# A ConvFFN over 2176 tokens: blocks of 724, 726 and 726 tokens become blocks of 868, 870 and 438

## The chip, the cores and the metric

One core of one Trainium2 chip runs the whole kernel in one launch. The metric is the device time of that launch in microseconds (us); smaller is better. Each execution of a kernel gives one time, and one further execution is profiled.

## The reference

One step of a one-layer encoder over 2048 prompt tokens and 8 x 16 sample tokens (2176 columns together), width 1024, in float32. Only the end of it is touched:

```
mix = concat(RMSNorm(A), RMSNorm(B)) @ w_out ;  x += RMSNorm(mix)
up = RMSNorm(x) @ w_up                 # 1024 -> 2 x 2816
up_c = causal depthwise conv (width 3) of up, + bias
f = (gelu(up_c[:2816]) * up_c[2816:]) @ w_down      # 2816 -> 1024
x += RMSNorm(f)
```

## The kernel before

Activations lie with features on the 128 partitions and tokens along the free axis, so a matmul takes a 128x128 weight tile as the stationary operand and a chunk of tokens as columns of the moving one. Each float32 operand is split into a high and a low part, and a product is three matmuls (hi·hi, lo·hi, hi·lo; `mm3`, L266 to L269). Every weight tile goes through `weights` (L174): a DMA from the SP queue into `wr` (two buffers), a cast on ScalarE (ACT) to `whi` (L184), a subtraction on VectorE (DVE) to `wlo` (L185); three weight buffers, two jobs of prefetch.

The stages are: the input projection with chunks of 384 and 512 columns; attention and gating; the output projection of six pieces of up to 384 tokens (48 jobs, `psm`); the ConvFFN. In the output projection two of the eight weight tiles (`KEEP`) stay resident over all six pieces, and the others are loaded again for each. For pieces 0 and 1 a chain there (`h2_chain`) also makes the normed input `hhi`, `hlo` of the first FFN block.

The FFN runs three blocks one after the other. A block has 44 up jobs (22 gate tiles, 22 value tiles, interleaved; 8 k-steps, two column chunks, three matmuls each) and down jobs in groups: when the 22 products `g` of a group are there, each of the 8 output tiles `m` adds its partial sum into `acc` (`down`, L1116). A job's two chunks go into the two `pd` buffers of PSUM, and DVE adds them into `acc` (L1139), so that the job after next needs these adds. The last up job of a block is followed by three down jobs of the fourth group and the eight of the last.

The input of block 1 and of block 2 is made by `ffn_prep_chain` (L871): first sums of squares, long ahead; then, once the last up job no longer reads `hhi`, for each sub-chunk of 182 columns a load of x1 into the single buffer `xp` (L880), eight products on DVE (L899), eight casts on ACT (`hhi`, L902), eight subtractions (`hlo`, L903), half on DVE and half on GpSimd (POOL). The next sub-chunk's load must wait until the last subtraction has read `xp`. The result of a block is normed, added to x1 (`xr`) and stored by `y_chain`, while the next block's up jobs run; the last block has `y_last_chain`, with its last group split into 470 and 256 columns so that the first part's chain runs beside the second part's matmuls.

A list scheduler lays out each engine's instructions from the program's order and its own estimates; each engine then runs its own list strictly in order.

Of the kernel before, what the change touches and what calls it, by code (L numbers as in the profile page):

```python
# [53 lines left out]
def hybrid_kernel(ctx: ExitStack, tc: tile.TileContext, a: dict):  # L54
# [194 lines left out]
    def sq_step(pool, key, acc, src, first, n, eng=None):  # L249
# [3 lines left out]
        else:  # L253
            sq = pool.tile([P, TAIL if key == "y" else 384], F32, tag="sq1" + key, name="sq1", bufs=2)
# [616 lines left out]
    def ffn_prep_chain(pool, pspool, fb, out, free):  # L871

        s0, n0, n1 = FBLK[fb]
        subs = [(o, min(182, n0 + n1 - o)) for o in range(0, n0 + n1, 182)]
        rbs = pool.tile([P, 728], F32, tag="rbs", name="rbs", bufs=1)
# [17 lines left out]
        hhi = hpool.tile([P, KD, 728], F32R, tag="hhi", name="hhi")  # L893
        hlo = hpool.tile([P, KD, 728], F32R, tag="hlo", name="hlo")
        for i, (off, n) in enumerate(subs):
            x, nxt = nxt, fetch_x1(*subs[i + 1]) if i + 1 < len(subs) else None
            for k in range(KD):
# [5 lines left out]
                (nc.gpsimd if k % 2 else nc.vector).tensor_tensor(out=lo, in0=x[:, k, :n], in1=hi.bitcast(F32),  # L903
                                                                  op=ALU.subtract)
# [6 lines left out]
    with ExitStack() as c3:  # L911
# [34 lines left out]
        def x1_chain(pi, mix, acc):  # L946
# [13 lines left out]
            if pi < 2:  # L960
                sumb = two.tile([P, 384], F32, tag="dgb", name="sumb", bufs=1)
            for k in range(KD):
# [10 lines left out]
                if pi < 2:  # L973
                    sq_step(two, "x", sumb, mix[:, k, :n], k == 0, n, nc.vector)
            held.discard("x")
            if pi < 2:
                chains.append(h2_chain(pi, mix, sumb))

        def h2_chain(pi, mix, acc):
# [5 lines left out]
            rb = (yield from rstd_chain(two, ps3s, "b", acc, n, D))[1]  # L985
# [47 lines left out]
        KEEP = (0, 2)  # L1033
        h2 += [hpool.tile([P, KD, 728], F32R, tag=t, name=t) for t in ("hhi", "hlo")]
# [14 lines left out]
    with ExitStack() as c4:  # L1049
# [8 lines left out]
        C0 = 150  # L1058
        NT = 726

        def block_jobs(fb, h2, h2n):
            s0, n0, n1 = FBLK[fb]
            first = fb == 0
            st = {}

            def up(f, w):
# [5 lines left out]
                segs = [(ps[:, 512 - n0:512], 0, n0), (ps[:, 512:512 + n1], n0, n1)]  # L1072
# [5 lines left out]
                if f == 2 * NF - 1:  # L1078
                    st["up"] = True
                    if h2n is None:  # L1080
                        x = st["x"] = hpool.tile([P, KD, 728], F32R, tag="hhi", name="xl").bitcast(F32)
# [5 lines left out]
                y = (ypool if first and f == 0 else two).tile([P, NT], F32, tag="yg" if f < NF else "yv", name="y")  # L1087
# [28 lines left out]
            def down(f0, G, m, parts, w):  # L1116
                dhi, dlo = w
                if f0 == 0 and m == 0:
                    st["acc"] = one.tile([P, KD, NT], F32, tag="acc", name="acc")
# [13 lines left out]
                for pi, pd, c in zip(parts, pds, cs):  # L1133
# [6 lines left out]
                    if last:  # L1140
                        if m == 0:
                            st["sum", pi] = one.tile([P, TAIL], F32, tag=f"sumy{pi}", name="sumy")
# [176 lines left out]
```

## Time and profile before

| | |
|---|---|
| three timed runs | 2992.3, 2996.45, 2998.28 us; median 2996.45 us |
| profiled execution | 2994.85 us, its span 2993.1 us (1.75 us lie around the span) |
| mean granted TensorE clock | 0.986 of full |
| TensorE (PE) busy | 2865.8 us, 96% of the span |
| FFN in the span | from about 1378 us to the end |
| weight tiles loaded | output projection 38, up 132, down 120 |

Span means from the first instruction to the last. PE's busy time counts a stretch as busy while a matmul is anywhere in its pipeline; matmuls overlap, so the distance from one start to the next, not the length of one, says what a matmul costs.

### The profile page before, as it was taken

How to read it: one execution, taken by the hardware profiler on the slowest of the kernel's cores; microseconds unless marked ns; L12 is line 12 of the kernel's file. 1: busy time of each engine (PE TensorE's matmuls, PEld its weight loads, DVE VectorE, ACT ScalarE, POOL GpSimd, SP SyncE). 2: the span in 40 equal slices, each digit the busy share in tenths (PEclk: the TensorE clock that was granted, in tenths of full speed). 3: DMA queues.
4: the chain of work that ended last, by engine and by line, in shares of the span. 5: the costliest groups of instructions: out<-in, count | busy, mean ns of one | idle time of the engine just before them, and what ended most of it. 6: DMA issues, size and time to landing. Idle time of an engine off the chain costs nothing.

```text
span 2993.1 us, 44225 instructions
## 1 busy us (share of the span) xinstructions
PE 2865.8 (96%) x17070; PEld 2620.6 (88%) x17070; DVE 1899.7 (63%) x2848; ACT 1354.4 (45%) x2399; POOL 343.1 (11%) x487
## 2 busy tenths in 40 slices
PE   8999978889999988999999999999999999999997
PEld 7999766567676657999999999899999999999997
DVE  6666658887988895876544555763444476344445
ACT  5444447777777774554332233433232243323222
POOL 0000011110111121552000000310000030000002
PEclk9999989999999999999999999999999999999998
DMA  7766864333424326665222212442212233211223
GB/s 241 243 232 232 253 205 127 117 100 82 120 85 113 106 60 205 211 206 184 79 68 72 64 61 75 150 123 76 69 50 71 63 111 117 77 58 59 75 64 109
DMA packets 241521, 360.26 MB, mean 120 GB/s; under 512 B 26400, under 2 KB 171040, under 8 KB 240288
## 3 DMA queue, kind: packets, MB, share of 16 engines
q1 hardware_dynamic: 241312, 357.44, 38.6%
q8 instruction: 135, 2.21, 0.3%
q14 instruction: 74, 0.61, 0.1%
HBM read 289.85 MB, written 67.51 MB: 119 GB/s over the span
## 4 chain that ended last, share of the span: by engine, by line
PE 56%; DVE 3%; DMA 2%; issue 1%; ACT 1%; POOL 0%; SPq 0%; POOLq 0%; DVEq 0%; ACTq 0%
PE pu L268 12%; PE pu L269 12%; PE pu L267 12%; PE pd L267 5%; PE pd L268 5%; PE pd L269 5%; PE psm L267 2%; PE psm L269 2%; PE psm L268 1%; DMA xp<-x_s 1%; DMA wr<-wout 1%; DVE xp L899 1%; DVE wlo L185 0%; PE rb L209 0%; PE rb L236 0%
## 5 line engine op out<-in xcount | busy, mean ns | idle before, releaser
L185 DVE TENSOR_TENSOR wlo<-wr,whi 128x1024 fp32r<-128x1024 f32 (+2 forms) x333 | 364.1, 1094 | 575.8 <-ACT whi L184 573.4
L267 PE MATMUL pu<-hhi,whi 128*128 128x364 f32 (+1 forms) x2112 | 694.8, 329 | 1.0 <-ACT nhs L1103 1.0
L268 PE MATMUL pu<-hlo,whi 128*128 128x364 f32 (+1 forms) x2112 | 695.5, 329 | 0.0
L269 PE MATMUL pu<-hhi,wlo 128*128 128x364 f32 (+1 forms) x2112 | 694.9, 329 | 0.0
L184 ACT CAST whi<-wr 128x1024 fp32r<-128x1024 f32 (+2 forms) x333 | 305.1, 916 | 726.3 <-PE pu L268 275.5
L267 PEld LDWEIGHTS pu<-hhi,whi 128*128 128x128 f32 x2112 | 398.6, 189 | 1.5 <-ACT nhs L1103 1.5
L268 PEld LDWEIGHTS pu<-hlo,whi 128*128 128x128 f32 x2112 | 398.0, 188 | 0.4 <-POOL hlo L903 0.3
L269 PEld LDWEIGHTS pu<-hhi,wlo 128*128 128x128 f32 x2112 | 397.5, 188 | 0.1
L267 PE MATMUL pd<-ghi,whi 128*128 128x362 f32 (+3 forms) x1016 | 335.2, 330 | 12.2 <-DVE acc L1139 11.5
L269 PE MATMUL pd<-ghi,wlo 128*128 128x362 f32 (+3 forms) x1016 | 334.1, 329 | 0.0
L268 PE MATMUL pd<-glo,whi 128*128 128x362 f32 (+3 forms) x1016 | 334.1, 329 | 0.0
L1091 DVE SCALAR_TENSOR_TENSOR y<-pu,cvec,y 128x726 f32<-128x726 f32 (+2 forms) x352 | 269.9, 777 | 8.7 <-ACT y L1088 4.1
L535 DVE TENSOR_TENSOR_SCAN S<-S 128x896 f32<-128x896 f32 (+8 forms) x136 | 216.3, 1594 | 24.4 <-ACT S L532 23.9
L532 ACT ACTIVATE S<-z 128x512 f32<-128x512 f32 (+4 forms) x336 | 189.0, 566 | 69.8 <-PE z L669 24.8
L686 PEld LDWEIGHTS pt<-ident,s 128*128 128x128 f32 x1088 | 126.6, 145 | 93.5 <-issue 34.8
L669 PE MATMUL z<-K,Q 128*128 128x512 f32 (+3 forms) x640 | 199.1, 408 | 8.7 <-ACT s L533 6.5
L267 PEld LDWEIGHTS pd<-ghi,whi 128*128 128x128 f32 x1016 | 191.9, 189 | 15.9 <-DVE acc L1139 8.0
L686 PE MATMUL pt<-ident,s 128*128 128x128 f32 x1088 | 176.8, 288 | 28.3 <-ACT wT L687 15.9
L1139 DVE TENSOR_TENSOR acc<-acc,pd 128x362 f32<-128x362 f32 (+2 forms) x192 | 101.5, 530 | 154.9 <-PE pd L269 154.3
L537 DVE TENSOR_TENSOR s<-s,S 128x640 f32<-128x640 f32 (+7 forms) x200 | 179.3, 901 | 27.6 <-ACT s L533 13.8
L268 PEld LDWEIGHTS pd<-glo,whi 128*128 128x128 f32 x1016 | 191.7, 189 | 0.3
L269 PEld LDWEIGHTS pd<-ghi,wlo 128*128 128x128 f32 x1016 | 191.4, 188 | 0.3
(210 smaller groups left out, 4913.8 us busy)
## 6 DMA issues: line engine op xcount, KB each, us to landing
wr<-wup SPq DMA_DIRECT2D x132, 512.0 KB, 3.3
wk<-win_t SPq DMA_DIRECT2D x96, 256.0 KB, 2.7
wr<-win_f SPq DMA_DIRECT2D x48, 512.0 KB, 5.3
wr<-wout SPq DMA_DIRECT2D x38, 512.0 KB, 3.9
wr<-wdown SPq DMA_DIRECT2D x72, 256.0 KB, 2.7
Q<-q_s SPq DMA_DIRECT2D x128, 128.0 KB, 5.1
x<-xT SPq DMA_DIRECT2D x40, 384.0 KB, 5.2
wr<-wdown SPq DMA_DIRECT2D x48, 320.0 KB, 2.9
```

The source lines that it names most:

```text
L184: nc.scalar.copy(hi, wr)
L185: nc.vector.tensor_tensor(out=lo, in0=wr, in1=hi.bitcast(F32), op=ALU.subtract)
L267: nc.tensor.matmul(ps, lhsT=whi, rhs=ahi, start=start, stop=False)
L268: nc.tensor.matmul(ps, lhsT=whi, rhs=alo, start=False, stop=False)
L269: nc.tensor.matmul(ps, lhsT=wlo, rhs=ahi, start=False, stop=stop)
L532: nc.scalar.activation(S[:, c0:c0 + cn], z, AF.Sigmoid, scale=-1.0)
L535: nc.vector.tensor_tensor_scan(out=R, data0=R, data1=R, initial=1.0 if carry is None else carry, op0=ALU.mult, op1=ALU.bypass)
L537: nc.vector.tensor_tensor(out=s[:, :W], in0=s[:, :W], in1=S[:, 1:W + 1], op=ALU.mult)
L669: nc.tensor.matmul(z, lhsT=Q[:, j, i * P:(i + 1) * P], rhs=K2[:, b0 * P + c0:b0 * P + c0 + cn], start=(j == 0), stop=(j == 1 and not diago ...
L686: nc.tensor.transpose(pt[:, j], st["w"][:, (j0 - b0 + j) * P:(j0 - b0 + j + 1) * P], ident)
L1091: nc.vector.scalar_tensor_tensor(out=o, in0=i, scalar=w, in1=o, op0=ALU.mult, op1=ALU.add)
L1139: nc.vector.tensor_tensor(out=o, in0=o, in1=src, op=ALU.add)
```

## The change

The FFN's blocks become 868, 870 and 438 tokens wide. In columns that PE multiplies by (with two halo or pad columns in each block) they are 434 + 436, 436 + 436 and 440 in a single chunk; before they were 362 + 364, 364 + 364 and 364 + 364. Both make 2182 columns. The down projection goes in six groups (4, 4, 4, 4, 3, 3 tiles) instead of five (5, 5, 4, 4, 4). The wider tiles take room: the gate's output `yg` has one buffer instead of two, `g` six instead of eight, `xr` three instead of four, and one output weight tile stays resident instead of two. Since the first block is wider, piece 2 of the output projection also makes 100 columns of its input. The prep's sub-chunks are five of 176 (the last 168) for block 1 and three of 148 (the last 144) for block 2, and all of `hlo` is made on POOL. The last group's parts are 256 and 182 columns.

```diff
-FBLK = [(0, 362, 364), (722, 364, 364), (1448, 364, 364)]
+FBLK = [(0, 434, 436), (866, 436, 436), (1736, 440, 0)]
+WB = 872
-FGROUPS = [5, 5, 4, 4, 4]
+FGROUPS = [4, 4, 4, 4, 3, 3]
-TAIL = 470
+TAIL = 256
+WY = 436
...
-        subs = [(o, min(182, n0 + n1 - o)) for o in range(0, n0 + n1, 182)]
+        total = n0 + n1
+        step = 2 * -(-total // (2 * -(-total // 182)))
+        subs = [(o, min(step, total - o)) for o in range(0, total, step)]
...
-                (nc.gpsimd if k % 2 else nc.vector).tensor_tensor(out=lo, in0=x[:, k, :n], in1=hi.bitcast(F32),
-                                                                  op=ALU.subtract)
+                nc.gpsimd.tensor_tensor(out=lo, in0=x[:, k, :n], in1=hi.bitcast(F32), op=ALU.subtract)
...
-            if pi < 2:
+            if pi < 3:
                 chains.append(h2_chain(pi, mix, sumb))
...
-        KEEP = (0, 2)
+        KEEP = (0,)
...
-                segs = [(ps[:, 512 - n0:512], 0, n0), (ps[:, 512:512 + n1], n0, n1)]
+                segs = [(ps[:, base:base + n0], 0, n0)] + ([(ps[:, 512:512 + n1], n0, n1)] if n1 else [])
...
-                y = (ypool if first and f == 0 else two).tile([P, NT], F32, tag="yg" if f < NF else "yv", name="y")
+                y = (ypool if f < NF else two).tile([P, WB - 2], F32, tag="yg" if f < NF else "yv", name="y")[:, :NT]
...
-                    st["g", f - NF] = split(two, y, [P, NT], "g", bufs=8)
+                    ghl = [two.tile([P, WB - 2], F32R, tag="g" + t, name="g" + t, bufs=6)[:, :NT] for t in ("hi", "lo")]
...
-                CS = [slice(0, 362), slice(362, NT)]
+                CS = [slice(0, n0), slice(n0, NT)] if n1 else [slice(0, NT)]
...
-                    xr = two.tile([P, 364], F32, tag="xr", name="xr", bufs=4)
+                    xr = two.tile([P, WY], F32, tag="xr", name="xr", bufs=3)
```

What the scheduler makes of it is seen where the first block ends and the second's input is prepared. On DVE, before, from one product of the second sub-chunk (`xp`) to the first products of the third, with `acc` the adds that free a `pd` buffer:

```order
L899 SCALAR_TENSOR_TENSOR xp<-xp,cvec,rbs 128x182
L1139 TENSOR_TENSOR acc<-acc,pd 128x364
L903 TENSOR_TENSOR hlo<-xp,hhi 128x182
L899 SCALAR_TENSOR_TENSOR xp<-xp,cvec,rbs 128x182
L185 TENSOR_TENSOR wlo<-wr,whi 128x512
L903 TENSOR_TENSOR hlo<-xp,hhi 128x182
L899 SCALAR_TENSOR_TENSOR xp<-xp,cvec,rbs 128x182
L1139 TENSOR_TENSOR acc<-acc,pd 128x362
L1139 TENSOR_TENSOR acc<-acc,pd 128x364
L185 TENSOR_TENSOR wlo<-wr,whi 128x512
L1139 TENSOR_TENSOR acc<-acc,pd 128x362
L899 SCALAR_TENSOR_TENSOR xp<-xp,cvec,rbs 128x182 x4
```

In the changed kernel, on DVE, from the second sub-chunk of the five to the third:

```order
L1147 TENSOR_TENSOR acc<-acc,pd 128x434
L904 SCALAR_TENSOR_TENSOR xp<-xp,cvec,rbs 128x176 x8
L1147 TENSOR_TENSOR acc<-acc,pd 128x436
L188 TENSOR_TENSOR wlo<-wr,whi 128x384
L1147 TENSOR_TENSOR acc<-acc,pd 128x434
L1147 TENSOR_TENSOR acc<-acc,pd 128x436
L188 TENSOR_TENSOR wlo<-wr,whi 128x384
L1147 TENSOR_TENSOR acc<-acc,pd 128x434
L1147 TENSOR_TENSOR acc<-acc,pd 128x436
L904 SCALAR_TENSOR_TENSOR xp<-xp,cvec,rbs 128x176 x8
```

The subtractions have left DVE, and the eight products of a sub-chunk stand together; from one sub-chunk's start to the next there are five `acc` adds, where before there were four. Counting on in the same list, there are five from the third to the fourth sub-chunk and three from the fourth to the fifth, which follows the block's last add.

On POOL, at the same place, the last three rows of the prep in the changed kernel with what stands around them (`sumy` is the sum of squares of the block's result, `rstd` its reciprocal root, which needs the block's last down job):

```order
L908 TENSOR_TENSOR hlo<-xp,hhi 128x176 x8
L259 TENSOR_TENSOR sumy<-sumy,sq_18842 128x436
L219 TENSOR_TENSOR rstd<-var,mhalf 128x4
L908 TENSOR_TENSOR hlo<-xp,hhi 128x168 x8
L219 TENSOR_TENSOR rstd<-var,mhalf 128x2
```

Before, the last rows there were these:

```order
L903 TENSOR_TENSOR hlo<-xp,hhi 128x182 x3
L256 TENSOR_TENSOR sumy<-sumy,sq_18605 128x362
L903 TENSOR_TENSOR hlo<-xp,hhi 128x182
L256 TENSOR_TENSOR sumy<-sumy,sq_18609 128x364
L216 TENSOR_TENSOR rstd<-var,mhalf 128x3
```

The fifth sub-chunk now stands behind the `rstd` of the finished block; before, the last sub-chunk was ahead of it.

On PE, the end of the first block before (`pd` are down jobs; `pu` are up jobs, here of the second block):

```order
L269 MATMUL pd<-ghi,wlo 128x362
L267 MATMUL pu<-hhi,whi 128x364
L267 MATMUL pd<-ghi,whi 128x364
L268 MATMUL pd<-glo,whi 128x364
```

And in the changed kernel, with the sums of squares of the finished block (`rb<-ones,sumy`):

```order
L271 MATMUL pd<-glo,whi 128x436
L272 MATMUL pd<-ghi,wlo 128x436
L272 MATMUL pu<-hhi,wlo 128x436
L212 MATMUL rb<-ones,sumy 128x64 x4
L270 MATMUL pu<-hhi,whi 128x436 x2
```

Before, up matmuls of the second block over all of its columns stood ahead of the last down jobs. Now only those over its first 436 columns do, and the first that read the second 436 columns (the last row shown) follow the `sumy` matmuls.

## Rows read from the trace of the kernel before

**Rows 1.** The page: the span.

```profile
span 2993.1 us, 44225 instructions
```

**Rows 2.** Windows in the FFN, PE alone: busy, matmuls, granted clock, DMA.

```profile
1500.00:1800.00 300.00, 300.00 (x1802) 1.00 0.22 66
2000.00:2400.00 400.00, 400.00 (x2406) 1.00 0.22 67
2500.00:2900.00 400.00, 400.00 (x2403) 1.00 0.23 72
```

**Rows 3.** Groups by shape, PE: count of the first of three matmuls.

```profile
L267 PE MATMUL pu<-hhi,whi 128*128 128x364 f32 x1760 | 578.4, 329 | 0.0
...
L267 PE MATMUL pd<-ghi,whi 128*128 128x364 f32 x496 | 164.0, 331 | 5.9 <-DVE acc L1139 5.9
...
L267 PE MATMUL pu<-hhi,whi 128*128 128x362 f32 x352 | 116.4, 331 | 1.0 <-ACT nhs L1103 1.0
```

**Rows 4.** Timeline of PE, last group: 34 starts at 470 columns, 36 at 256.

```profile
2953.49 0.37 PE L269 MATMUL pd<-ghi,wlo 128*128 128x470 f32 x1
...
2960.59 0.38 PE L269 MATMUL pd<-ghi,wlo 128*128 128x470 f32 x1
2960.80 0.28 PE L267 MATMUL pd<-ghi,wl 128*128 128x256 f32 x1
...
2964.98 0.28 PE L269 MATMUL pd<-ghi,wl 128*128 128x256 f32 x1
```

**Rows 5.** Timeline of PE, earlier stages: 55 starts at 512 columns; 97 at 384.

```profile
99.29 0.39 PE L396 MATMUL pst<-wklo,hhi 128*128 128x512 f32 x1
...
111.53 0.39 PE L396 MATMUL pst<-wklo,hhi 128*128 128x512 f32 x1
...
118.13 0.33 PE L267 MATMUL psf<-hhi,whi 128*128 128x384 f32 x1
...
134.77 0.34 PE L267 MATMUL psf<-hhi,whi 128*128 128x384 f32 x1
```

**Rows 6.** Timeline of PE in the gating stage: eight starts at 512 columns.

```profile
923.18 0.40 PE L820 MATMUL pu<-uw,xl 128*128 128x512 f32 x1
...
924.80 0.40 PE L818 MATMUL pu<-uw,xh 128*128 128x512 f32 x1
```

**Rows 7.** Who PE waited for in the FFN: us, times, longest.

```profile
PE pd L267 <- DVE acc L1139: 11.5, 9, 2.7
```

**Rows 8.** Windows at the two block borders, PE alone.

```profile
1850.00:1910.00 60.00, 53.55 (x317) 1.00 0.42 123
2385.00:2450.00 65.00, 59.28 (x351) 1.00 0.33 102
```

**Rows 9.** Timelines of SP and DVE at the first border: load, landing, next load.

```profile
1865.52 0.38 SPq L880 DMA_DIRECT2D xp<-x_s  x1
...
1877.97 0.38 SPq L880 DMA_DIRECT2D xp<-x_s  x1
...
1870.36 1.64 DVE L899 SCALAR_TENSOR_TENSOR xp<-xp,cvec,rbs 128x182 f32<-128x182 f32 x4 [1.11 <-DMA xp<-x_s]
```

**Rows 10.** All subtractions of the prep by engine: shortest, median, longest in ns.

```profile
L903 DVE TENSOR_TENSOR hlo<-xp,hhi x32: 331/341/741, 1853.5 to 2440.6; 128x182 fp32r<-128x182 f32 x32
L903 POOL TENSOR_TENSOR hlo<-xp,hhi x32: 505/582/1559, 1854.6 to 2442.6; 128x182 fp32r<-128x182 f32 x32
```

**Rows 11.** Output projection: window (PE, PEld, DVE, ACT, POOL busy), then instructions added to it.

```profile
1158.00:1378.00 220.00, 214.67 (x1288) 209.39 (x1288) 158.52 (x249) 113.54 (x218) 115.36 (x108) 0.99 0.63 211
...
L185 DVE TENSOR_TENSOR wlo<-wr,whi x37: 1208/1226/2037, 1169.4 to 1370.7; 128x1024 fp32r<-128x1024 f32 x37
...
L256 DVE TENSOR_TENSOR sumb<-sumb,sq x14: 545/560/1365, 1205.0 to 1259.8; 128x384 f32<-128x384 f32 x14
```

**Rows 12.** The page's DMA issues: down weights, KB each, us to landing.

```profile
wr<-wdown SPq DMA_DIRECT2D x72, 256.0 KB, 2.7
```

**Rows 13.** The last window: PE, PEld, DVE, ACT, POOL busy, clock, DMA.

```profile
2973.00:2993.10 20.10, 2.85 (x15) 1.90 (x13) 15.70 (x31) 0.74 (x2) 7.96 (x10) 0.61 0.40 148
```

More of the change, by code (lines that the diff above doesn't have):

```diff
@@ L892, in ffn_prep_chain @@
             yield
-        hhi = hpool.tile([P, KD, 728], F32R, tag="hhi", name="hhi")
-        hlo = hpool.tile([P, KD, 728], F32R, tag="hlo", name="hlo")
+        hhi = hpool.tile([P, KD, WB], F32R, tag="hhi", name="hhi")
+        hlo = hpool.tile([P, KD, WB], F32R, tag="hlo", name="hlo")
         for i, (off, n) in enumerate(subs):
@@ L984, in h2_chain @@
             yield
-            rb = (yield from rstd_chain(two, ps3s, "b", acc, n, D))[1]
+            rb = (yield from rstd_chain(two, ps3s, "b", acc, max(n, P), D))[1]
             parts = [(0, 0, NSAMP), (NSAMP, NSAMP + 2, n - NSAMP)] if pi == 0 else [(0, c0 + 2, n)]
@@ L1031, in wout @@
             return resident[m]
-        KEEP = (0, 2)
-        h2 += [hpool.tile([P, KD, 728], F32R, tag=t, name=t) for t in ("hhi", "hlo")]
+        KEEP = (0,)
+        h2 += [hpool.tile([P, KD, WB], F32R, tag=t, name=t) for t in ("hhi", "hlo")]
         for t in h2:
@@ L1064, in block_jobs @@
             st = {}
+            NT = n0 + n1 if first else n0 + n1 - 2
+            base = 512 - n0 if n1 else 0
+            C0 = base if first else base + 2
             def up(f, w):
@@ L1118, in down @@
                 if f0 == 0 and m == 0:
[L1119 removed]
+                    st["acc"] = one.tile([P, KD, WB - 2], F32, tag="acc", name="acc")
                 acc = st["acc"]
                 last = f0 + G == NF
[L1122 removed]
+                CS = [slice(0, n0), slice(n0, NT)] if n1 else [slice(0, NT)]
                 if last and h2n is None:
@@ L1141, in down @@
                         if m == 0:
-                            st["sum", pi] = one.tile([P, TAIL], F32, tag=f"sumy{pi}", name="sumy")
+                            st["sum", pi] = one.tile([P, WY], F32, tag=f"sumy{pi}", name="sumy")
                         sq_step(two, "y", st["sum", pi], o, m == 0, n, nc.vector if m == KD - 1 else None)
@@ L1147, in down_job @@
             def down_job(f0, G, m):
-                return (lambda: weights(a["wdown"][m][:, f0:f0 + G])), (lambda w: down(f0, G, m, (0, 1), w))
+                return (lambda: weights(a["wdown"][m][:, f0:f0 + G])), (lambda w: down(f0, G, m, (0, 1) if n1 else (0,), w))
             def last_job(f0, G, m, pi):
@@ L1168, in y_last_chain @@
                 x, t0 = st["x"], s0 + 2 + c0
-                rb = (yield from rstd_chain(one, psd, "yb"[pi], ssum, n, D, w=(TAIL, 256)[pi]))[1]
+                rb = (yield from rstd_chain(one, psd, "yb"[pi], ssum, n, D, w=TAIL))[1]
                 for k in range(KD):
@@ L1185, in y_chain @@
                 yield from lock("y")
-                rb = (yield from rstd_chain(one, psd, "y", ssum, n, D, w=TAIL))[1]
+                rb = (yield from rstd_chain(one, psd, "y", ssum, n, D, w=WY))[1]
                 if first:
```

19 lines of the change are left out of this document (10 added, 9 removed).

## The prediction

> **What bounds the kernel now.** The windows come first: three undisturbed stretches of the FFN, 1100 us of the span [rows 1], in which PE is busy all the time at the full granted clock [rows 2]. They hold 1802 + 2406 + 2403 = 6611 starts, so a matmul costs 1100/6611 = 166.4 ns there from one start to the next. The reader is to see that nothing but the number of matmuls and this distance sets the FFN's time. The groups by shape give the number: 1760 + 352 = 2112 first matmuls of up jobs [rows 3], three matmuls each, so 6336; the down jobs are 22 tiles x 8 outputs x 3 matmuls x 2 chunks x 3 blocks = 3168 (496 of the first kind at 364 columns in the same rows, as many at 362, and 64 in the last split). Together 9504 at 363.6 columns. At 2.4 GHz, the level that the granted clock of 1.00 stands for, 363.6 columns are 151.5 ns, so 14.9 ns of a matmul do not go by columns. Next the list of waits: what PE loses in the FFN is mostly the wait of down jobs for `acc`, 11.5 us in nine waits [rows 7], and the windows put the loss at the two block borders: 60 - 53.55 = 6.45 us and 65 - 59.28 = 5.72 us, 12.2 together [rows 8].
>
> **The change part by part.**
>
> *Fewer, wider matmuls.* The columns stay (2182 for up, 2178 for down), the matmuls fall: up 44 x 24 x 5 = 5280, down 22 x 24 x 5 = 2640, and 72 more for the split of the last group: 7992, or 1512 fewer. No row has 436 columns, so the distance is bounded by its neighbours. At 470 columns it is 7.10 us/33 = 215.2 ns, at 256 4.18/35 = 119.4 ns [rows 4]. At 512 it is 12.24/54 = 226.7 ns, at 384 16.64/96 = 173.3 ns [rows 5], but at 512 in the gating stage 1.62/7 = 231.4 ns [rows 6]. Less the columns at 2.4 GHz these are 19.3 ns at 470, 12.8 at 256, 13.3 at 512 and 384, 18.1 at 512 in gating: the part that does not go by columns is no constant. It is smallest where chunk and tile sizes are multiples of 64 columns, and largest at the wide odd ones. 436 is odd, so I lean to that side. For 435.9 columns the mean is then: 195.0 ns with 13.3 ns; 196.5 with the 14.9 of now; 198.1 on the line from 166.4 at 363.6 to 231.4 at 512; 199.6 on the line to 215.2 at 470; 201.0 with the 19.3 of 470. I take 198.1. Before: (9504 - 192) x 0.1664 + 96 x 0.2152 + 96 x 0.1194 = 1581.6 us. After: (7992 - 144) x 0.1981 + 72 x 0.1194 + 72 x 0.09 = 1569.8 us (182 columns lie between 182/2.4 = 75.8 ns and the 119.4 of 256; the middle). **-12 us**, ends -36 (195.0) and +11 (201.0).
>
> The Trainium skill, TensorE: Matmul & The Clock Gate, section Back-to-back issue gap, gives the isolated distance as columns/2.4 plus 2.5 ns; by it 1512 fewer matmuls would return 3.8 us. The distances above do not agree with it: what stands beside the columns is 13 to 19 ns here, so its figure is not used.
>
> *Block borders.* At the first border a load of `xp` goes out at 1865.52 us, its first product starts at 1870.36, and the next load goes out at 1877.97 [rows 9]: a sub-chunk takes 12.4 us, of which 4.8 are the load. DVE's list puts the first product of a sub-chunk ahead of `acc` adds, so while DVE waits for the load, PE runs out of `pd` buffers. Between two such products there were four adds, two down jobs of 24 x 0.1664 = 4.0 us: 12.4 against 8.0. Now there are five adds, 2.5 jobs of 18 x 0.198 = 3.6 us = 8.9 us, and a sub-chunk is a little shorter in loading (176 columns). What grows is the number of sub-chunks for block 1, five for four, with 11 down jobs beside them that last 11 x 3.6 = 39 us instead of 44. All subtractions now run on POOL: 8 x 0.582 = 4.7 us a sub-chunk, where DVE did four at 0.341 [rows 10]; with the load (4.8) and a first product and cast ahead (about 1, an estimate from the 0.4 us that a product takes in the same row group 9: four in 1.64) that is 10.5 us, and more where `sumy` adds stand between. I walk it: from the end of the last up job (0), loads go out at about 15 (as before, DVE has the tile's last elementwise work first), 25, 35.5 and 46.5; the waits of PE for `acc` are about 3.0, 2.2 and 0.8 us; the fifth sub-chunk lands at 51, and its first `hlo` is there at about 52, where the down jobs and the six matmuls ahead of the second half of the columns would have ended at 41 without any wait. So about 11 us are lost at the first border, 4.5 more than now. At the second border there are three sub-chunks: loads at about 12 and 22, waits of 3.7 and 2.4 us, and the third is there long before the down jobs end: 6.1 against 5.7. **+5 us**; below, 0 (the longer DVE list hides it as well as now); above, +13 (the fifth sub-chunk at 12.4 us each and not at 10.5: four times 1.9 us more).
>
> *Output projection.* One more weight tile loaded for five pieces: 5 x 1.23 us on DVE. Eight more squares and sums at 0.56 us each, and 100 columns of `h` and `hlo` for eight k. DVE is busy 158.5 of 220 us and PE 214.7 [rows 11], so PE has 5.3 us of idle time there and DVE 61 us of room for some 6 + 4.5 + 4 us. **+2 us**; ends 0 (all in the room) and +8 (half of the added DVE work delays a weight tile).
>
> *Third block.* One chunk, so an up job lasts 24 x 0.2 = 4.8 us and a down job 12 x 0.2 = 2.4 us, where a down job had 4 to 5 us. A down tile needs 2.7 us from issue to landing [rows 12], and two `wr` buffers and two jobs of lead (4.8 us) cover it. The one place where it is thin is the first down group, beside which SP also issues the loads and stores of `xr` for the second block, now with three buffers. **+1 us**; ends 0 and +8 (eight jobs short by 1 us).
>
> *Tail.* After the last matmul come 20.1 us, of which DVE works 15.7 [rows 13]. The last block's parts shrink from 470 and 256 columns to 256 and 182, so its elementwise work shrinks by 438/726, but the second part's matmuls hide 6.5 us of it instead of 11.5: 15.7 x 0.4 = 6.3 less, 5.0 more, **-2 us** with the shorter chain of four pieces instead of six; ends 0 and -5.
>
> *At nothing:* the single gate buffer (a value job's product on DVE is done many us before the next gate tile's 48 matmuls end, cover 9.5 us, and 4.8 in the third block), six `g` buffers (3 + 3 or 4 + 1 tiles live), 24 more down loads of the same total bytes.
>
> Sum: -12 + 5 + 2 + 1 - 2 = -6 us. The profiled execution took 2994.85, so 2989; the median of the timed runs lies 1.6 above it: **2990 us**.
>
> **The rivals.**
>
> *The width pays in full.* If the part beside the columns stays at the 14.9 ns of now, or falls to 13.3, the first term is -24 to -36, and with the rest at +6 the kernel takes 2979 to 2967. For it: 362 and 364 are odd too and have no more. Against: 470 and 512 in gating. Chance 0.20.
>
> *The width pays nothing* (the other side). If 436 columns cost like 470 (199.6 to 201.0 ns), the first term is 0 to +11 and the kernel takes 3002 to 3013; it decides from about 199.4 ns on. For it: 470 is the nearest wide row. Against: those are 96 matmuls of one place. Chance 0.17.
>
> *The fifth sub-chunk becomes the border.* POOL's subtractions go up to 1.56 us [rows 10] and the last sub-chunk stands behind `rstd`, so each step may take 12.4 us or more; at +13 to +20 for the border the kernel takes 2998 to 3005. The Trainium skill, GPSIMD Engine Reference, section Engine selection, advises VectorE for two-input elementwise work and puts GpSimd at about twice its time; the medians above, 582 to 341 ns, bear it out at 1.7. Chance 0.13.
>
> *The change doesn't reach PE:* short jobs of the third block starve (weights late by 1 us in each of 24 down jobs or more), which eats the gain: 2998 to 3010. For it: two loads in flight only; against: all three stages of a tile take less than its lead. Chance 0.10.
>
> **How the numbers follow.** The forecast (a net of -2 to -12) has 0.40. A measurement of this kernel tells 0.2%, 6 us, from no change; the forecast lies at that edge, so half of its chance is faster and half the same. Faster is 0.20 and the first rival's 0.20. Of the other three a part ends within 6 us: same is 0.20 + 0.06 + 0.06 + 0.04 = 0.36, slower 0.11 + 0.07 + 0.06 = 0.24. The range leaves out the ends of the first rival below and of the second and fourth above: 2973 to 3004. The forecast's own range is 2984 to 2994.
>
> **What the profile after would show.** Windows inside the blocks with 100/0.198 = 505 starts in 100 us (513 if the first rival holds, 498 if the second); 5280 up and 2712 down matmuls in three lines; PE losing about 11 us at the first border, the last piece of it on `hhi` or `hlo` of the fifth sub-chunk, and about 6 at the second; 43 output weight tiles; a last window of some 18 us. Wrong I would be above all by the distance at 436 columns: a nanosecond there is 7.8 us.

## The result

The changed kernel takes 3021.02 us (median of 4 timed runs, 3015.88 to 3024.86), the kernel before 2994.38 us beside it: ratio 1.0081, 95% interval 1.0069 to 1.0093, or +24 us. The forecast was 2990 with a range up to 3004, so it missed in direction and by 31 us. The profiled execution took 3024.86 us, the slowest of the four; its span is 30.0 us longer than that of before [rows 1].

The page of the changed kernel, span and DMA issues (KB each, us to landing):

```profile
span 3023.1 us, 41499 instructions
...
wr<-wdown SPq DMA_DIRECT2D x96, 256.0 KB, 2.7
wr<-wout SPq DMA_DIRECT2D x43, 512.0 KB, 4.6
...
wr<-wdown SPq DMA_DIRECT2D x48, 192.0 KB, 2.4
```

Windows of the changed kernel, PE alone (busy, starts, granted clock, DMA), in undisturbed stretches of the FFN, to be read against [rows 2]:

```profile
1500.00:1900.00 400.00, 400.00 (x2023) 1.00 0.20 60
2100.00:2600.00 500.00, 500.00 (x2531) 1.00 0.21 63
2760.00:2940.00 180.00, 180.00 (x901) 1.00 0.36 107
```

The reader is to see the cadence: 400/2023 and 500/2531 are 197.7 ns per start, 180/901 (440 columns) 199.8. The forecast was 198.1. The wide matmuls do what was said of them, and the loss must lie elsewhere.

Windows of the same kernel at the two borders, the first jobs of the third block, the last group, and behind the last matmul (the last row has PE, PEld, DVE, ACT and POOL):

```profile
1960.00:2060.00 100.00, 87.52 (x400) 0.90 0.35 104
2610.00:2680.00 70.00, 63.47 (x321) 1.00 0.26 75
2680.00:2750.00 70.00, 64.72 (x324) 1.00 0.60 185
2975.00:3009.00 34.00, 30.15 (x199) 0.95 0.32 101
...
3009.00:3023.00 14.00, 1.69 (x7) 1.10 (x6) 9.64 (x29) 0.71 (x2) 5.81 (x10) 0.66 0.38 128
```

At the first border there are 400 starts in 100 us; at 197.7 ns they are worth 79 us, so 21 us are gone, and only 12.5 of them are idle time. Most of the rest (6.0 us, by the table below) stands in the clock: 0.90, where [rows 8] have 1.00. The lists of waits of PE in the output projection, at the first border, at the second with the third block's start, and in the last group (us, times, longest):

```profile
PE psm L270 <- ACT mix L1020: 4.4, 2, 2.3
PE rb L239 <- DVE dg L231: 4.2, 3, 1.9
...
PE pd L270 <- DVE acc L1147: 10.3, 4, 3.3
PE pu L270 <- ACT hhi L907: 1.3, 1, 1.3
PE rb L212 <- DVE sumy L259: 0.9, 1, 0.9
...
PE pd L270 <- DVE acc L1147: 6.5, 3, 2.7
PE pu L270 <- ACT nhp L1110: 2.6, 2, 1.6
PE pd L270 <- ACT acc L1145: 1.7, 1, 1.7
...
PE pd L270 <- ACT wl L187: 3.5, 3, 2.2
```

The timeline of DVE at the first border: the eight products of sub-chunks 2 to 5, and one of the adds behind them.

```profile
1990.27 5.21 DVE L904 SCALAR_TENSOR_TENSOR xp<-xp,cvec,rbs 128x176 f32<-128x176 f32 x8 [0.48 <-DMA xp<-x_s]
1995.40 0.59 DVE L1147 TENSOR_TENSOR acc<-acc,pd 128x436 f32<-128x436 f32 x1
...
2003.80 4.56 DVE L904 SCALAR_TENSOR_TENSOR xp<-xp,cvec,rbs 128x176 f32<-128x176 f32 x8
...
2018.11 5.76 DVE L904 SCALAR_TENSOR_TENSOR xp<-xp,cvec,rbs 128x176 f32<-128x176 f32 x8 [0.23 <-DMA xp<-x_s]
...
2031.78 3.84 DVE L904 SCALAR_TENSOR_TENSOR xp<-xp,cvec,rbs 128x168 f32<-128x168 f32 x8 [0.30 <-DMA xp<-x_s]
```

A sub-chunk takes 13.5, 14.3 and 13.7 us from one to the next, where the prediction walked with 10.5. The timeline of PE beside it:

```profile
1996.05 0.48 PE L270 MATMUL pd<-ghi,whi 128*128 128x436 f32 x1 [3.31 <-DVE acc L1147]
...
1998.14 0.57 PE L270 MATMUL pd<-ghi,whi 128*128 128x436 f32 x1
1998.50 0.57 PE L271 MATMUL pd<-glo,whi 128*128 128x436 f32 x1
...
2000.69 0.36 PE L270 MATMUL pd<-ghi,whi 128*128 128x434 f32 x1
2000.88 0.36 PE L271 MATMUL pd<-glo,whi 128*128 128x434 f32 x1
...
2009.86 0.55 PE L270 MATMUL pd<-ghi,whi 128*128 128x434 f32 x1 [3.02 <-DVE acc L1147]
...
2032.59 1.09 PE L270 MATMUL pu<-hhi,whi 128*128 128x436 f32 x2 [1.31 <-ACT hhi L907]
```

PE waits 3.3 us until the eight products let the add through, and then its matmuls start 0.36 us apart (1998.14 to 1998.50), at the lower of the two clock levels, before they are back at 0.19. The second half of the columns starts at 2032.59, when the fifth sub-chunk's `hhi` is there.

To add this up by place, the trace of each kernel was read in one way: for each FFN matmul, the distance to the next start less the usual one for its columns (columns at 2.4 GHz plus 15 ns), where that is over 40 ns. In brackets is the part in matmuls at the lower clock level. The output projection is the time from the start of the last matmul of the stage ahead to that of its own last.

| us | vs before | output proj. | FFN start | border 1 | border 2 | third block's start | last group | after the last matmul |
|---|---|---|---|---|---|---|---|---|
| before | | 223.8 | 2.2 | 8.7 (0.0) | 7.4 (0.0) | 0.3 | 0.8 | 19.4 |
| changed | +24 | 231.0 | 5.4 | 22.6 (6.0) | 9.6 (0.0) | 5.1 | 7.8 (1.6) | 14.3 |
| before, POOL alone | +8 | 225.4 | 2.3 | 13.3 (3.0) | 12.4 (2.7) | 0.3 | 0.7 | 19.1 |
| before, reload alone | +4 | 230.2 | 4.1 | 8.3 (0.0) | 9.7 (1.5) | 0.3 | 0.7 | 19.0 |
| before, groups alone | +26 | 224.7 | 2.1 | 18.1 (2.5) | 16.3 (2.7) | 0.3 | 6.7 (1.7) | 19.1 |
| changed, old widths | +26 | 226.9 | 5.3 | 18.6 (4.5) | 16.3 (2.9) | 0.3 | 6.6 (1.6) | 19.0 |
| changed, half on DVE | +29 | 230.0 | 3.1 | 22.1 (2.3) | 11.2 (1.5) | 8.2 | 10.1 | 14.8 |
| changed, 16 jobs | +18 | 230.0 | 3.2 | 17.6 (5.5) | 6.4 (1.5) | 7.4 | 7.4 | 14.5 |
| changed, two `xp` | +13 | 229.6 | 5.4 | 11.0 (0.0) | 7.2 (0.0) | 5.1 | 7.7 | 14.5 |
| changed, all three | +4 | 231.9 | 3.0 | 7.4 (0.3) | 4.5 (0.2) | 7.2 | 7.1 | 14.5 |
| old widths, all three | +10 | 225.2 | 3.2 | 13.7 (0.0) | 8.5 (0.0) | 0.3 | 4.9 | 19.0 |
| before, 16 jobs, two `xp` | -14 | 225.1 | 2.3 | 4.1 (0.0) | 1.2 (0.0) | 0.6 | 1.0 | 18.8 |

Of the 30.0 us between the spans 3.9 lie ahead of the output projection, where the code is the same (that point was reached at 1131 to 1144 us in all profiles). The FFN, from the last matmul of the output projection to the last of its own, grew from 1612.7 to 1636.7: +24.0, of which stalls are 52.3 - 20.3 = +32.0, so the matmuls themselves gave back 8.0.

### The profile page after: what moved, and what is told of

Its sections match the earlier page's. It is cut to its first block, busy times and chain, and to the rows that moved or that the text cites. A ratio compares the mean times of both kernels' runs of the same rounds, so it can differ in the third digit from the quotient of the medians.

```text
span 3023.1 us, 41499 instructions
## 1 busy us (share of the span) xinstructions
PE 2881.4 (95%) x15566; PEld 2549.3 (84%) x15566; DVE 1926.9 (64%) x2886; ACT 1364.9 (45%) x2436; POOL 367.8 (12%) x524
## 4 chain that ended last, share of the span: by engine, by line
PE 51%; DVE 5%; DMA 4%; ACT 1%; issue 1%; POOL 1%; SPq 0%; DVEq 0%; POOLq 0%; ACTq 0%
PE pu L271 11%; PE pu L270 11%; PE pu L272 11%; PE pd L270 5%; PE pd L272 5%; PE pd L271 5%; DVE wlo L188 1%; DMA wr<-wout 1%; DVE xp L904 1%; DMA xp<-x_s 1%; PE psm L270 1%; PE psm L272 1%; PE psm L271 1%; ACT whi L187 1%; DVE mix L967 1%
## 5 line engine op out<-in xcount | busy, mean ns | idle before, releaser
L270 PE MATMUL pu<-hhi,whi 128*128 128x434 f32 (+2 forms) x1760 | 636.7, 362 | 6.0 <-ACT nhp L1110 2.6
L271 PE MATMUL pu<-hlo,whi 128*128 128x434 f32 (+2 forms) x1760 | 638.0, 362 | 0.0
L272 PE MATMUL pu<-hhi,wlo 128*128 128x434 f32 (+2 forms) x1760 | 636.5, 362 | 1.1 <-DVE wlo L188 1.1
L270 PE MATMUL pd<-ghi,whi 128*128 128x436 f32 (+2 forms) x856 | 312.1, 365 | 18.6 <-DVE acc L1147 16.8
L272 PE MATMUL pd<-ghi,wlo 128*128 128x436 f32 (+2 forms) x856 | 310.4, 363 | 0.0
L271 PE MATMUL pd<-glo,whi 128*128 128x436 f32 (+2 forms) x856 | 310.1, 362 | 0.0
L1096 DVE SCALAR_TENSOR_TENSOR y<-pu,cvec,y 128x740 f32<-128x740 f32 (+3 forms) x352 | 270.0, 778 | 15.1 <-ACT y L1093 10.9
L690 ACT COPY wT<-pt 128x512 f32<-128x512 f32 (+3 forms) x320 | 164.3, 551 | 63.2 <-PE pt L689 60.9
L706 PE MATMUL po<-wT,V 128*64 128x256 f32 (+1 forms) x1152 | 188.8, 389 | 3.3 <-ACT wT L690 3.0
L536 ACT ACTIVATE s<-z 128x512 f32<-128x512 f32 (+4 forms) x336 | 189.1, 568 | 0.0
```

Source lines behind the costliest of these rows:

```text
L270: nc.tensor.matmul(ps, lhsT=whi, rhs=ahi, start=start, stop=False)
L271: nc.tensor.matmul(ps, lhsT=whi, rhs=alo, start=False, stop=False)
L272: nc.tensor.matmul(ps, lhsT=wlo, rhs=ahi, start=False, stop=stop)
L536: nc.scalar.activation(s[:, c0:c0 + cn], z, AF.Sigmoid)
L706: nc.tensor.matmul(po[gg * 64:gg * 64 + 64, q], lhsT=shared["V"][:, j, gg * 64:(gg + 1) * 64], rhs=T[:, (j - b0) % 4, q], start=first_, st ...
L1096: nc.vector.scalar_tensor_tensor(out=o, in0=i, scalar=w, in1=o, op0=ALU.mult, op1=ALU.add)
```

## The experiments

All are compared with the kernel before, on the same chip; the ratio stands with its 95% interval.

**Half of the subtractions back on DVE**, in the changed kernel:

```diff
-                nc.gpsimd.tensor_tensor(out=lo, ...)
+                (nc.gpsimd if k % 2 else nc.vector).tensor_tensor(out=lo, ...)
```

> The changed kernel with one thing undone: every second subtraction of the prep is on DVE again. Theory A (POOL): at the first border the eight products of a sub-chunk stand together on DVE and take 5.2 us, 0.65 us each, because POOL subtracts at the same time (0.38 us each where POOL is idle); the acc adds behind them come late, PE waits about 3 us per sub-chunk and its clock falls to 1.2 GHz after it. With half of the subtractions back, products take 0.4 us, DVE's piece per sub-chunk is 8 x 0.4 + 4 x 0.34 = 4.6 us, the waits shrink by some 0.6 us each and the clock falls less: 3010 to 3017. Theory B (number of sub-chunks): the border is long because five sub-chunks follow one another beside 11 shorter down jobs; who subtracts matters little: 3018 to 3023.

Measured 1.0097 (1.0083 to 1.0111), +29, at the upper end of theory B or just above it. Theory A fails as a cause by itself: the products are quick again and PE waits less for `acc` (7.0 us instead of 10.3), but the border loses 22.1, as in the changed kernel, because PE then waits for `sumy` (5.5) and the fifth sub-chunk (`hhi` 2.8 us). The part of it at the lower clock falls from 6.0 to 2.3 us, and that returns nothing either. The start of the last up matmul, the first products of the fifth sub-chunk and the start of the second half of the columns:

```profile
1965.64 0.36 PE L272 MATMUL pu<-hhi,wlo 128*128 128x436 f32 x1
...
2025.08 1.31 DVE L904 SCALAR_TENSOR_TENSOR xp<-xp,cvec,rbs 128x168 f32<-128x168 f32 x4 [3.49 <-DMA xp<-x_s]
...
2025.89 1.10 PE L270 MATMUL pu<-hhi,whi 128*128 128x436 f32 x2 [2.80 <-ACT hhi L907]
```

The fifth sub-chunk starts 59.4 us after the last up matmul, against 60.5 in the changed kernel: quick products, with half of the subtractions beside them on DVE, hardly shorten the chain.

**All subtractions on POOL**, in the kernel before: the reverse edit there.

> The kernel before with one part of the change alone: all subtractions of the prep on POOL. Theory A: the four sub-chunks' products stand together on DVE and slow down to 0.65 us, as in the changed kernel; both borders lose 2 to 5 us more: 2998 to 3005. Theory B: no change, 2992 to 2997.

Measured 1.0027 (1.0016 to 1.0038), +8: theory A. The move costs by itself, at both borders, though the chain gets shorter (the last subtraction of the first border ends 49.8 us after the last up matmul, against 53.9). The products by tile `xp` (shortest, median, longest in ns) of before, of this run and of the run above:

```profile
L899 DVE SCALAR_TENSOR_TENSOR xp<-xp,cvec,rbs x32: 392/403/1125, 1851.8 to 1901.2; 128x182 f32<-128x182 f32 x32
```

```profile
L899 DVE SCALAR_TENSOR_TENSOR xp<-xp,cvec,rbs x32: 395/647/1134, 1852.5 to 1897.8; 128x182 f32<-128x182 f32 x32
```

```profile
L904 DVE SCALAR_TENSOR_TENSOR xp<-xp,cvec,rbs x40: 388/395/1314, 1966.9 to 2028.8; 128x176 f32<-128x176 f32 x32, 128x168 f32<-128x168 f32 x8
```

**Sixteen down jobs behind the last up job**, in the changed kernel:

```diff
-                    jobs += pairs[0] + prev[:5]
-                    for p in pairs[1:]:
-                        jobs += p
-                    jobs += prev[5:]
+                    for p in pairs:
+                        jobs += p
+                    jobs += prev
```

> The changed kernel with the eight down jobs of the last group but one all behind the block's last up job (16 down jobs stand there, not 11). Theory A: the waits for acc at the borders stay (about 10 and 6 us), since they come from DVE's list and not from the end of the jobs; only the last block's tail gains, because its last eight weight tiles have 8 x 9 x 0.2 = 14 us of matmuls ahead of them instead of 5.4: its 7 us of stalls go, 3012 to 3017. Theory B: 18 us more of cover take the border's loss as well: 2998 to 3008.

Measured 1.0061 (1.0048 to 1.0075), +18: the time of theory A, but not for its reason. The waits for `acc` stay, at 9.6 us, as it said; but the two borders lose 5 and 3 us less, and the last group, from which it had the gain, does not gain.

**One resident weight tile less**, in the kernel before (`KEEP = (0,)`):

> The kernel before with one resident output weight tile less, nothing else. The stage of the output projection lasted 11 us longer in the changed kernel. Theory C (the reload): five more tiles with cast and subtraction delay the stage by most of that: 3000 to 3005. Theory D (the third chain that makes the input of block 0, or the tiles' other places): 2993 to 2997.

Measured 1.0014 (1.0005 to 1.0023), +4, between the two ranges; the stage itself is 6 us longer, which speaks for theory C.

**Half on DVE and 16 jobs together:**

> The changed kernel with both edits of the first runs at once: half of the prep's subtractions on DVE, and 16 down jobs behind the last up job. One alone gave +29 us against the kernel before, the other +18, the changed kernel +24. Theory E (two bounds in a row at the first border): the chain of five sub-chunks sets when the second half of the columns can start, and DVE's list makes PE wait on the way; either edit alone leaves the other bound. Together the 22 us lost there fall to about 10: +9 to +14 us against the kernel before. Rival (the edits add up): +29 + 18 - 24 = +23.

Measured 1.0057 (1.0038 to 1.0075), +17, between theory and rival: border 1 fell to 13.3, not 10, and border 2 stayed at 8.6.

**The last group's weights asked for at once**, in the changed kernel:

```diff
-                        st["w", m] = weights(a["wdown"][m][:, f0:f0 + G], out=out)
+                        for mm in range(KD) if m == 0 else ():
...
+                            st["w", mm] = weights(a["wdown"][mm][:, f0:f0 + G], out=out)
```

> The changed kernel with the last group's eight weight tiles asked for at once, two jobs ahead of the first, instead of each two jobs ahead of its own. Theory F (lead): in the last group a job of 256 columns and nine matmuls lasts 1.07 us, two of them 2.1, and a tile needs 2.4 us to land and some 0.9 for cast and subtraction, so each tile comes late; asked for at once they flow, and the 6.9 us of stalls there fall to 1 to 3: +18 to +21 us against the kernel before. Rival (rate): two landing buffers and the cast give a tile every 1.6 us at best whenever it is asked for: +23 to +25.

Measured 1.0081 (1.0059 to 1.0103): no change, 7.3 us of stalls instead of 7.8, as the rival had it. But the loads did not go out earlier: the third to sixth of the eight tiles leave SP 1.4, 2.0, 9.2 and 10.2 us after the last up matmul in both kernels. So the run says that asking earlier in the program does not help, not that an earlier tile would not.

**Two resident tiles in the changed kernel**, with one buffer for `h`:

> The changed kernel with two resident output weight tiles again; the room comes from the tile h of the chain that makes block 0's input, which has one buffer here. In the kernel before the reload alone cost +4. Theory C (the reload is a part of the output projection's 11 us, the third chain the rest): +19 to +21 against the kernel before. Theory D (the third chain is all of it here, or the single h buffer costs as much as the reload): +23 to +28.

Measured 1.0142 (1.0124 to 1.0160), +43, outside both: the output projection takes 249.5 us, with pieces of 9.4 and 7.8 us in which PE stands. The single `h` became the wait, so this run says nothing of the reload. It shows how near the chain that makes block 0's input is to the path.

**All edits so far**, with two `xp` paid for by two `xr`:

> All of the edits together on the changed kernel: half of the subtractions on DVE, 16 down jobs behind the last up job, the last group's weights asked for at once, two resident output weight tiles, and two buffers for xp (xr then has two). If the stalls are what ate the 11 us that the wider matmuls return, and each edit takes its part (border 10 to 14, tail 4 to 6, output projection 4), the kernel comes to -2 to +5 us against the kernel before. If the wider matmuls return nothing, it stays at +8 or more.

Measured 1.0131 (1.0114 to 1.0148), +39: the same `h` (249.8 us), and one wait of 14.4 us at the third block's start, where the first down jobs need the `acc` that `y_chain`, short of `xr`, still holds. Border 1 however lost only 7.1.

**Without the third chain:** the squares and `h2_chain` only for `pi < 2` again.

> The changed kernel without the third chain: piece 2 of the output projection doesn't make its 100 columns of block 0's input, which stay zero here (this part is left out). Theory G (the third chain holds the buffer mix longer, so the copies of piece 4 out of PSUM come late and PE waits; with its own squares and products it is the other half of the 11 us): the stage ends about 5 us earlier, +18 to +20 us against the kernel before, the changed kernel stands at +24. Rival (the reload and the tiles' other places are all of it): +23 to +25.

Measured 1.0066 (1.0051 to 1.0080), +20; the output projection falls from 231.0 to 224.3. Theory G, though the interval overlaps that of the changed kernel, so the stage's own time carries the reading.

**All three border edits:** half on DVE, 16 jobs, two `xp`, paid for by one `yv`.

```diff
-            x = pool.tile([P, KD, 182], F32, tag="xp", name="xp")
+            x = pool.tile([P, KD, 182], F32, tag="xp", name="xp", bufs=2)
...
-                y = (ypool if f < NF else two).tile(..., tag="yg" if f < NF else "yv", name="y")[:, :NT]
+                y = (ypool if f < NF else two).tile(..., tag="yg" if f < NF else "yv", name="y", bufs=1)[:, :NT]
```

> The changed kernel with half of the subtractions on DVE, 16 down jobs behind the last up job, and two buffers for xp (the value tile yv has one for it, xr keeps three). In the run with all edits the first border lost 6 us by starts and the second 4, against 22 and 8 in the changed kernel and 13 and 9 with the first two edits alone. Theory E (the chain of sub-chunks, loads included, is the bound at the border): the same here, +5 to +10 us against the kernel before. Rival (the single yv buffer makes value jobs wait, or a third stall takes its place): +14 or more.

Measured 1.0013 (1.0004 to 1.0021), +4: theory E. 20 of the 24 us were at the borders.

**And two resident tiles, paid for by one `sumx`,** with the last group's weights asked for at once:

> The border edits of the run beside it, two resident output weight tiles with the room from a single buffer for the sums of squares sumx, and the last group's weights asked for at once. If the reload costs here what it cost in the kernel before (+4) and nothing waits for sumx: 4 to 5 us less than the run beside it, 0 to +6 against the kernel before. If sumx becomes a wait as the tile h did (+18 there): +15 or more.

Measured 1.0010 (1.0001 to 1.0019), +3, not told from the run beside it: the stage takes 230.1 with two resident tiles as well. Without the third chain it took 224.3 with one, and the two runs below with the old widths, which have one resident tile and no third chain either, take 226.9 and 225.2. So in the changed kernel it is the third chain that brings the stage to 230, and the second resident tile is worth 2 us at most; why the same reload made the stage 6 us longer in the kernel before stays open.

**The kernel before with 16 jobs and two `xp`:**

> The kernel before with two of the border edits: two buffers for xp, 16 down jobs behind the last up job. Its borders lose 8 and 7 us by starts. Theory E: most of that goes, -6 to -11 us against the kernel before. Rival (in the kernel before the loss is DVE's list, the adds behind the products, which stay): -2 to +2.

Measured 0.9954 (0.9941 to 0.9967), 2985.37 us, -14: faster than both kernels, and beyond the -11 of theory E (the interval reaches up to -10). Its windows at the borders, PE alone, against [rows 8]:

```profile
1825.00:1925.00 100.00, 97.72 (x590) 1.00 0.44 131
2360.00:2430.00 70.00, 69.48 (x414) 1.00 0.29 86
```

**The changed kernel with the old widths:**

```diff
-FBLK = [(0, 434, 436), (866, 436, 436), (1736, 440, 0)]
+FBLK = [(0, 362, 364), (722, 364, 364), (1448, 364, 364)]
-WB = 872
+WB = 728
-TAIL = 256
+TAIL = 470
```

> The changed kernel with the widths of before (blocks of 724, 726 and 726 tokens in chunks of 362 and 364, last group split 470 and 256, two chains in the output projection), and all else of the change left in: one resident weight tile less, all subtractions on POOL, six down groups, single gate buffer, six g, three xr. Theory H (the wide blocks cost by themselves: the cadence gives 11 us back, and the fifth sub-chunk, the third chain, the short third block and the short last group take 20 or more): what is left is the reload (+4 alone) and POOL (+8 alone), so +10 to +14 us against the kernel before, half of the changed kernel's +24. Rival (the groups and the fewer buffers are what costs): +18 to +24.

Measured 1.0085 (1.0072 to 1.0099), +26: the rival, a little beyond its range. The wide blocks neither gain nor cost here; what came with them costs it all.

**Two `xp` (and one `yv`) alone**, in the changed kernel:

> The changed kernel with two buffers for xp (and one for yv) alone. With half of the subtractions on DVE and 16 down jobs as well, this step took 13 us. Theory E (the chain of five sub-chunks is the bound, and each waits for its load): 10 to 13 us here too, +11 to +14 against the kernel before. Rival (it only helps once there are 16 down jobs): +20 to +24.

Measured 1.0044 (1.0032 to 1.0057), +13: theory E. Border 1 falls to 11.0, in nine waits of at most 1.5 us, at a clock of 1.00. The products are as slow as in the changed kernel (median 0.63 us), but the fifth sub-chunk starts 39.0 us after the last up matmul, where it was 60.5:

```profile
1970.96 0.36 PE L272 MATMUL pu<-hhi,wlo 128*128 128x436 f32 x1
...
2009.92 0.69 DVE L904 SCALAR_TENSOR_TENSOR xp<-xp,cvec,rbs 128x168 f32<-128x168 f32 x2
```

**Two `xp` alone in the kernel before:**

> The kernel before with two buffers for xp alone; with 16 down jobs as well it was 12.7 us faster than the kernel before. Theory E: the loads are most of it, -6 to -11 us. Rival (the 16 jobs are): -3 to +1.

Measured 0.9981 (0.9972 to 0.9990), -6, at the edge of theory E; by difference the 16 jobs give the other 8.

**The last group in one part of 438 columns:**

> The changed kernel with the last group in one part of 438 columns, not two of 256 and 182. Theory F (in the last group a job of 256 columns is shorter than what a weight tile takes): a job now lasts 1.8 us, and the 7 us of stalls there shrink to 2 or less; but nothing is left beside which the first part's chain could run, and what follows the last matmul grows from 14.3 us by 6 to 10. Net +24 to +29 against the kernel before. Rival (the stalls there have another cause, the late tile wl): stalls stay, +30 or more.

Measured 1.0088 (1.0075 to 1.0102), +26: theory F's account, 2.5 us of stalls instead of 7.8, and 20.3 after the last matmul instead of 14.3. Jobs that are shorter than a tile's turn in two `wr` buffers are thus a part of it; the rate itself was not measured alone. The next run shows a second part.

**The six groups alone**, in the kernel before:

```diff
-FGROUPS = [5, 5, 4, 4, 4]
+FGROUPS = [4, 4, 4, 4, 3, 3]
```

> The kernel before with the down projection in six groups (4, 4, 4, 4, 3, 3) and nothing else. With the widths of before, the rest of the change came to +25 us; the reload alone was +4, POOL alone +8. Theory I (cover): the 11 down jobs behind a block's last up job work on 33 tiles, not 44, 11 us less beside the same chain of sub-chunks; each border loses 3 to 5 us more, and the last group waits 3 to 5 us for its tiles: +9 to +15 us against the kernel before. Rival (the groups are harmless, the parts of the change only cost together): -2 to +4.

Measured 1.0087 (1.0073 to 1.0102), +26: theory I, and at twice the size. Windows at its borders and in its last group, PE alone, and who PE waits for at the first border:

```profile
1860.00:1960.00 100.00, 88.65 (x505) 0.97 0.41 126
2410.00:2480.00 70.00, 59.96 (x329) 0.95 0.30 93
2970.00:3006.00 36.00, 32.65 (x181) 0.95 0.29 101
```

```profile
PE pd L267 <- DVE acc L1139: 6.8, 7, 2.3
PE pu L268 <- DVE hlo L903: 1.9, 1, 1.9
PE pu L267 <- ACT hhi L902: 1.9, 1, 1.9
```

PE now waits for `hhi` and `hlo` of the next block as well as for `acc` [rows 7].

The last group loses 6.7 us here as well, though its first jobs, nine matmuls at 470 columns, last 1.94 us by [rows 4], longer than the 1.8 of the run before this one. Who PE waits for there, SP's list, and the landing of its two `wdown` loads:

```profile
PE pd L267 <- ACT wl L184: 3.1, 1, 3.1
...
2965.53 2.03 SPq L1084 DMA_DIRECT2D xl<-x_s  x4
2967.66 1.14 SPq L65 DMA_DIRECT2D wr<-wdown  x2
...
DMA to landing us min/median/max: 11.2/11.3/11.3
```

Once the last up job is done, SP loads x1 for the end of the block (`xl`, 2.9 MB), and the two weight tiles asked for behind it take 11.3 us to land. In the changed kernel `xl` is 1.75 MB and the two tiles behind it take 6.7 us, where the median of its `wdown` tiles of 192 KB is 2.4; the longest stall of its last group, 2.3 us, ends when the first of them has landed and been cast. Before, such tiles came as late (10.9 us), but the down jobs ahead of them had four tiles each and not three, and the group lost 0.8 us.

**Old widths with all three border edits:**

> The changed kernel with the widths of before and with the three border edits (half of the subtractions on DVE, 16 down jobs behind the last up job, two xp and one yv). The same edits with the wide blocks gave +4 us, and the kernel before with its own border cured -13. Theory J (wide blocks are worth nothing: 11 us of cadence and 5 of the tail against the third chain, the short third block and the short last group): 0 to +8. Theory K (with the border cured the wide blocks cost 8 us or more): -4 to -10. Theory L (they gain): +10 or more.

Measured 1.0033 (1.0023 to 1.0044), +10, the edge of theory L. The wide blocks with the same edits were at 1.0013 (1.0004 to 1.0021): once the borders are cured they are worth some 6 us.

## Why the prediction was wrong, step by step

**Fewer, wider matmuls (-12): right.** 197.7 ns, 199.8 in the third block, against 198.1; 8.0 us came back by the stage, and 10.2 by the forecast's own formula with these distances (6336 x 0.1977 + 1512 x 0.1998 + 72 x 0.1194 + 72 x 0.112 = 1571.4, from 1581.6). Both rivals on the distance, the width in full and the width for nothing, fall. That 198.1 was hit so closely owes something to luck: it was the middle of five values that ran from 195.0 to 201.0. The part beside the columns is some 16 ns at 434 and 436 columns and 16.5 at 440; that it is smallest at multiples of 64 was no sound reading, since 512 in the gating stage had 18.1.

**Block borders (+5): the step that failed.** Measured +13.9 and +2.2. The walk had the right bound at the first border, the end of five sub-chunks beside 11 down jobs, and it priced the difference: the fifth sub-chunk ready at 52 us, the down jobs done at 41 without any wait, 11 us lost. The down jobs were right (198 matmuls of 0.198 us are 39 us). What failed is the step from one sub-chunk to the next: 10.5 us in the walk, 13.5 to 14.3 measured. The loads went out 14.6, 25.7, 40.2 and 55.1 us after the last up matmul, not at 15, 25, 35.5 and 46.5, and the second half of the columns could start at 61.4 (1971.2 to 2032.6). 61.4 less 39 is the 22.6 us lost, nearly. Within a step the load took 4.3 to 6.2 us (4.8 in the walk), the way from the first product to the last subtraction 6.6 to 8.1 (5.7 in the walk), and once the products stood 2.3 us behind other work in DVE's list.

Only the subtractions were priced for POOL; the products on DVE were left at their 0.41 us, and they take 0.63 to 0.65 while POOL subtracts, with `acc` adds queued behind all eight. The Trainium skill, SBUF — State Buffer, section Who interferes with whom, states that a VectorE instruction with two inputs in SBUF contends with a GpSimd instruction that reads SBUF. This case's rows agree (403 ns to 647 by that move alone), and the forecast had cited only the rule on POOL's own speed. But the slow products are not what sets the chain's end: with half of the subtractions on DVE and quick products the fifth sub-chunk starts at 59.4 us instead of 60.5, and the border loses as much. The single `xp` is: with two buffers, and the products as slow, the fifth starts at 39.0, and the border loses 11.0.

The clock is a term that the sum did not have: 6.0 of the 22.6 us are matmuls at the lower level after waits of 2.9 to 3.3 us. At this border it is no cost on top, since with half on DVE it falls to 2.3 and PE waits for the end of the chain instead. As for the cover, the groups of three make the work behind the last up job 33 tiles where it was 44. At the old widths that is 33 us instead of 44, and alone it costs 9 us at each border. With the wide columns it is 39 us, as the prediction had it; what the groups cost in the wide kernel no run shows alone. Half of the subtractions on DVE, 16 jobs and two `xp`, which quicken the chain and lengthen its cover, return 20 us together; the first of them alone returns nothing.

**At nothing (groups, down loads): wrong.** The last group lost 7.0 us more. It is the mechanism of the fourth rival, late tiles, in a place that it did not name, and for two reasons: two of its tiles are loaded behind `xl` (6.7 us to land) with fewer matmuls ahead of them, and its jobs of nine matmuls at 256 columns last 1.07 us, where a tile of 192 KB needs 2.4 to land even when nothing is ahead of it. How the 7.0 divide between the two no run shows. At the FFN's start 3.2 us more are lost (0.8 to 1.0 in three other versions of the changed kernel in the table); that was not followed up.

**Third block (+1):** +4.8, at its first jobs, where PE waits for `nhp` (a `pu` buffer that ACT and DVE give back late while `y_chain` runs) and for `acc` of the second block. A job lasts 4.8 us there, and the elementwise work of the block before is still to be done beside it.

**Output projection (+2, up to +8):** +7.2, near its upper end. PE waits 4.4 us for copies into `mix`, which the third chain holds longer; without that chain the stage takes 224.3 us, as before.

**Tail (-2, down to -5):** -5.1, its lower end.

The sum by these steps: 7.2 + 3.2 + 13.9 + 2.2 + 4.8 + 7.0 - 8.0 - 5.1 = 25.2, and 0.9 in small stalls elsewhere: 26.1, which with the 3.9 ahead of the output projection is the 30.0 between the spans. The third rival, the fifth sub-chunk, had the right place and at +13 to +20 the right size. What it lacked were the others: each rival was priced with all else as forecast, and here four terms went the same way at once. In the borders, the third block and the last group the jobs that hide other work had become fewer or shorter; the output projection is another matter.

Shown by runs are the cost of the six groups and of POOL at the old widths, of the third chain and the single `xp` in the changed kernel, and that longer jobs take stalls from the last group. The reload costs in the kernel before alone. Single costs sum to more than the whole: 26 + 8 + 4 alone, and all three together at the old widths +26, with borders (18.6 and 16.3 us) hardly longer than the groups alone make them (18.1 and 16.3). How much of a border is the clock and how much the wait that precedes it was read from the rows, not tried alone; why the third block's start waits is an argument from who waits for whom.

## What to carry to other kernels

When a change regroups the work that hides a serial chain, write down for each place the length of the chain and the length of its cover, before and after, and price the difference as a wait; a group of three for a group of four cost more here than all the wide matmuls returned. Work that moves to POOL has a second price on DVE, if both read SBUF at the same time. See also what a queue has ahead of a late load: here a tile that lands in 2.4 us took 6.7 behind a large one. And first double the buffer in the chain and lengthen the cover in the kernel as it stands: here that gave 14 us without any change of widths.

## What the hardware showed that was not expected

A 182-column matmul is not paid by its columns. In the last group they start 0.11 us apart, where 182 columns at 2.4 GHz are 75.8 ns and the 256 of [rows 4] took 119.4.

```profile
3001.32 0.28 PE L270 MATMUL pd<-ghi,wl 128*128 128x182 f32 x1
3001.44 0.27 PE L271 MATMUL pd<-glo,wl 128*128 128x182 f32 x1
3001.55 0.27 PE L272 MATMUL pd<-ghi,wl 128*128 128x182 f32 x1
```

The clock falls after some waits and not after others. In the changed kernel four waits of 10.3 us, the longest 3.3, left a granted clock of 0.90 over the first border; with two `xp` nine waits of 8.3 us, none over 1.5, left it at 1.00, and so did the waits of before, the longest of them 2.7 [rows 7, 8]. The longest wait alone does not decide it: with the six groups alone the longest wait for `acc` at the first border was 2.3, in seven waits of 6.8 us, and the clock stood at 0.97. What does decide it these runs do not show.
